# Three reorderings in a fused hybrid layer: one projection block behind a weighted sum, the entry of the up-projection written out, and the first activation blocks of the down-projection ahead of a weight fetch

## The chip, the cores and the metric

One core of one Trainium2 chip. The metric is the device time of one execution in microseconds. An execution is told apart from its span: the span runs from the first to the last instruction that the profile shows, the execution is a little longer.

## What is computed

One layer of a streaming encoder, on 512 frames of width 1024, all in float32:

```python
h = rms_norm(x, mix_norm_pre)
xa, ga, q, k, v, f_logit, g_a, g_b = split(h @ w_in)
y_a = gelu(ga) * rg_lru(causal_dwconv(xa))                   # recurrent branch, width 1280
y_b = forgetting_attention(q, k, v, f_logit + b_forget)      # 16 heads of 64
merged = sigmoid(g_a + b0) * (y_a @ w_proj_a) + sigmoid(g_b + b1) * (y_b @ w_proj_b)
x = x + rms_norm(merged @ w_out, mix_norm_post)
h = rms_norm(x, ffn_norm_pre)
gate, val = split(causal_dwconv(h @ w_up))                   # 3 taps, 2 x 3072 channels
x = x + rms_norm((gelu(gate) * val) @ w_down, ffn_norm_post)
```

## The kernel before

**Products.** Each float32 operand is split into a high part, rounded to the matmul's type, and a low part, the remainder. ACT makes the high part (a cast, `hi`), DVE the low one (a subtraction, `lo`, `sub`), and PE adds three products (high x high, high x low, low x high) in one PSUM bank. Weights come by DMA on SP's queue into a buffer `raw`, of which there are four, and go through the same split into `wh` and `wl`. Since a buffer is taken in turn, a fetch on SP waits until the split of an earlier weight has been read, and every DMA that is queued on SP behind it waits with it.

**Attention.** Heads go in eight pairs, one a turn of the loop over `p`. A pair's scores are made on PE, normalised on DVE and ACT (`normalise`), turned by PE transposes into PSUM banks (`pt`, tiles pt and pt_r, two banks a head), split (PTh on ACT, PTl on DVE), and multiplied with v (`av`). The result lies in two banks, one a head; ACT copies half (ytmp), DVE adds (y), ACT rounds (yb, index 0), DVE takes the remainder (yb, index 1). Pair p's transposes and `av` come one turn later, in turn p + 1. In the last turn PE's time is filled with `pb_part(e, ks)`: block e of the product of y_b with `w_proj_b`, for the pairs ks. For each k it is three products that read yb of pair k, and it accumulates in bank pb e.

**Up-projection.** Pairs of weight blocks, one for the gate and one for the value (block j and j + 24), of which the first three (`NU`) are computed plainly and the rest, from j = 3 on, by a seven-product scheme on halves (class `Pair`): products 1, 2, 4 read plain weight quarters, 3 another plain quarter, 5, 6, 7 sums of quarters. A plain quarter's high part mh is a cast on ACT (`plain_high`). Its low part ml is made by ACT writing minus the high part (`plain_low`), after which a DMA that POOL issues adds the raw weight in place (line 360). `sums` are subtractions on DVE (t), `sums_hi` and `sums_lo` split them (th, tl). `keep(i, ps)` copies a bank's half to SBUF on ACT (x), since it is needed in a later sum; product 3 accumulates into the half that `keep(1)` reads, and product 6 into the one that `keep(2)` reads. From j = 3 on `period` gives the order of one pair's work by hand, with the preparation of the next two pairs (`n1`, `n2`) in between. The work ahead of the first period is written out by hand too; there `p` is pair 3, `n` pair 4, and pair 5 is prepared by the first period. The three plain pairs' convolution taps (`first_tap` on ACT, `first_taps` on DVE), gelu and product (`first_glu`: gelu on ACT, yf on POOL, stored to DRAM as yd by SP) stand in between.

**Down-projection.** 42 steps in seven products by six blocks of weights, `STEPS`, each of twelve matmuls of 128x512. A step needs weights (wh_dn, wl_dn) and activations (ah, al, made from yr or q). `load_w(i)` queues the fetch of step i's weights on SP, `load_q` that of a block q of activations from yd in DRAM (128x2x256 elements, half the bytes of a weight block). Steps 0 to 5 read yr; step 6, the first of product 4, reads the first q block, which `load_22(0)` loads. The q tiles lie in a pool that is opened after the up-projection's memory is given back (`ustk.close`). `extra[i]` is a list of what is done beside step i.

**Order.** In the parts under `manual_schedule` the order on each engine is the order of the code. Elsewhere a scheduler orders each engine's instructions, by estimates of its own; in the attention it does.

Of the kernel before, what the change touches and what calls it, by code (L numbers as in the profile page):

```python
# [19 lines left out]
KD = D // P  # L20
# [43 lines left out]
def kernel(  # L64
# [274 lines left out]
    class Pair:  # L339
# [14 lines left out]

        def plain_low(self, i):

            src = self.plain_src(i)
            l = self.ml[i] = self.split_tile(i, "ml")
            act.activation(out=l, in_=src, func=AF.Copy, scale=-1.0)  # L359
            nc.gpsimd.dma_start(l, src, accum_op=ALU.add)  # L360
# [2 lines left out]
            return (self.r[0], self.r[1][:, B])[i]  # L363

        def plain_high(self, i):
            src = self.plain_src(i)
            h = self.split_tile(i, "mh")
            act.copy(h, src)
            l = self.ml.get(i)
            if l is None:  # L370
                l = self.split_tile(i, "ml")
                sub(l, src, h.bitcast(F32))
            if i == 0:
                self.w[1], self.w[2] = quarter(h, l, A), quarter(h, l, B)
            else:
                self.w[3] = quarter(h, l, A)

        def plain(self, i):
            if i not in self.ml:
                self.plain_low(i)  # L380
                self.plain_high(i)

        def sums(self, i):
            r0, r1 = self.r
            t = self.t[i] = self.st.tpool.tile([P, D], F32, tag="t", name=self.name(f"t{i}"))
            if i == 0:
                sub(t[:, A], r1[:, A], r0[:, A])
                sub(t[:, B], r1[:, B], r1[:, A])
            else:
                sub(t[:, A], r1[:, B], self.t[0][:, A])  # L390
                sub(t[:, B], r0[:, B], t[:, A])
# [566 lines left out]
    with ExitStack() as at:  # L958
# [39 lines left out]
        def normalise(pts):  # L998
            for Pt, sm in pts:
                dve.reciprocal(sm, sm)  # L1000
                for b in (3, 2, 0, 1):
                    w = P * (b + 1)
                    dve.tensor_scalar(out=Pt[:, PO[b] : PO[b] + w], in0=Pt[:, PO[b] : PO[b] + w],
                                      scalar1=sm[:, b : b + 1], scalar2=None, op0=ALU.mult)
# [25 lines left out]
        def av(p, pts):  # L1030
            y = apool.tile([P, S], F32, tag="y", name=f"y{p}", bufs=2)
            tmp = apool.tile([P, S], F32, tag="ytmp", name=f"ytmp{p}", bufs=1)
            for j in range(2):
                th, tl = pts[j]
                po = bank(f"av{2 * p + j}")
                for kb in range(NT):
                    st = vt[p][:, kb, 2 * j : 2 * j + 2, :].rearrange("p a b -> p (a b)")
                    d = slice(PTO[kb], PTO[kb] + S - kb * P)
                    pe.matmul(po[:, kb * P :], st, th[:, d], start=kb == 0, stop=False)
                    pe.matmul(po[:, kb * P :], st, tl[:, d], start=False, stop=kb == NT - 1)  # L1040
                r = slice(HD * j, HD * (j + 1))
                o = slice(HD * (1 - j), HD * (2 - j))
                act.copy(tmp[r], po[o])
                dve.tensor_tensor(out=y[r], in0=po[r], in1=tmp[r], op=ALU.add)
            yb[p] = vpools[p // 4].tile([P, 2, S], F32R, tag="vy", name=f"yb{p}")
            act.copy(yb[p][:, 0], y)
            dve.tensor_tensor(out=yb[p][:, 1], in0=y, in1=yb[p][:, 0].bitcast(F32), op=ALU.subtract)
# [3 lines left out]
        def pb_part(e, ks):  # L1051
            if e not in pb:
                pb[e] = bank(f"pb{e}")
                pbw[e] = unit(f"pb{e}", 1)
            wh, wl = pbw[e]
            for k in ks:
                mm3(pb[e], wh[:, k], wl[:, k], yb[k][:, 0], yb[k][:, 1], k == 0, k == KD - 1)
# [9 lines left out]
        for p in range(KD):  # L1067
            if p == 0:
                pq = held("q1", 1)
            now = scores(p, q, k, bias)  # L1070
            if p < KD - 1:
                bias = prep_alloc(p + 1)
            if 0 < p < KD - 1:
                pq = bank(f"q{p + 1}")
                project(pq, (unit if p > 1 else behind)(f"q{p + 1}"), hh, hl)
            elif p:
                pb_part(0, range(KD - 2))
            if prev is not None:
                pts = pt(p - 1, prev)
            if p < KD - 1:  # L1080
                pk = bank(f"k{p + 1}")
                project(pk, behind(f"k{p + 1}", 2 if p else 0), hh, hl)
                q, k = halves(pq, f"q{p + 1}"), halves(pk, f"k{p + 1}")
            else:
                pb_part(1, range(KD - 2))
            if p == 0:
                b.product(4, b.a[:, Y])
                gate_epilogue(b, "a", 0)
                gate_epilogue(b, "a", 1)
            if prev is not None:  # L1090
                av(p - 1, pts)
            normalise(now)
            prev = now
        pts = pt(KD - 1, prev)
        for e in range(2):
            pb_part(e, range(KD - 2, KD - 1))
        pb_part(2, range(KD - 1))
        av(KD - 1, pts)

# [46 lines left out]
    def up_pair(j):  # L1146
        return Pair(ups, j, (f"up{j}", f"up{j + JF}"))
# [200 lines left out]
    first_tap(1)  # L1348
    first_taps(1)
    first_tap(2)  # L1350
    p.p12()
    n.sums_hi(0)
    n.sums_hi(1)
    n.plain(1)
    p.keep(2, p.a[:, Y])
    p.add(p.a[:, X], p.a[:, X], 2)
    pairs[NU + 2] = up_pair(NU + 2)
    p.p5()
    n.sums_lo(0)
    p.keep(1, p.c[:, X])  # L1360
    n.sums_lo(1)
    first_glu(1)
    first_tap(0)
    first_taps(2)
    first_taps(0, 0)
    PRODUCTS = (1, 4, 5, 6, 7, 3, 2)
    WQ = {1: (0, 0), 2: (1, 0), 3: (1, 1), 4: 3, 5: 0, 6: 1, 7: 2}
    STEPS = [(n, m) for n in PRODUCTS for m in range(NS)]
# [51 lines left out]
    pairs.update({j: none for j in (JF, JF + 1, JF + 2)})  # L1420

    def load(j):
        if j + 3 < JF:
            pairs[j + 3] = up_pair(j + 3)
        elif j == JF - 2:
            for i in range(2):
                load_w(i)
                load_first(i)

    with man2:  # L1430
# [20 lines left out]
        y_lo(0)  # L1451
        p.product(3, p.c[:, X])
        taps(b.j, b.a, b.g)
        gelu(b.g)
        wd[1].hi()
        y_hi(1)
        glu(b.j, b.g, b.v)
        p.product(7, p.a[:, Y])
        p.add(p.c[:, Y], p.a[:, Y], 1)
# [15 lines left out]
            load_w(i + 1)  # L1475
        down_step(1)
        down_step(2)
        load_w(7)
        prep(4)
        gelu(p.g)  # L1480
        glu(p.j, p.g, p.v)
# [72 lines left out]
        extra = {i: [] for i in range(len(STEPS))}  # L1554
        at_ = {n: NS * PRODUCTS.index(n) for n in PRODUCTS}
        gpost = dpool.tile([P, D], F32, name="gpost")
        for m in range(NS):
            for i, f, a in ((1, load_22, (m,)), (6, load_q, (1, 0, m)), (12, load_q, (0, 0, m)), (19, load_12, (m,)),
                            (8, s1, (m,)), (14, s2, (m,)), (20, s3, (m,)), (26, s4, (m,))):
                extra[max(3, i + m)].append(lambda f=f, a=a: f(*a))  # L1560
        extra[5].append(lambda: nc.sync.dma_start(gpost, gains[3:4, :].partition_broadcast(P)))
        extra[9].append(lambda: act.mul(gpost[:, DH:], gpost[:, DH:], -1.0))
        extra[9].append(lambda: act.activation(out=warm, in_=epst, func=AF.Sqrt))
# [142 lines left out]
```

## Time and profile before

| | us |
|---|---|
| median of 3 runs (lowest to highest) | 915.69 (915.38 to 916.62) |
| profiled execution | 916.23 |
| its span | 914.5 |
| PE matmul busy | 904.9 (99%) |
| DVE busy | 725.6 (79%) |
| ACT busy | 601.7 (66%) |
| POOL busy | 217.6 (24%) |

The page's busy time counts a matmul from its start to an end that is modelled, so that neighbours overlap: the start of one row and the start of the next say how fast PE goes. The TensorE clock was granted fully (0.998 on the mean). In the timeline a row is: start, us from there to the last end, engine, line, operation, output<-inputs, how many; in square brackets the idle time of the engine ahead of it and what ended that. PE is the matmul engine, DVE VectorE, ACT ScalarE, POOL GpSimd, SP SyncE; a "q" behind an engine's name marks its queue of DMAs.

### The profile page before, as it was taken

What the parts mean: (1) busy time and instruction counts of PE and PEld (TensorE: products, weight loads), DVE (VectorE), ACT (ScalarE), POOL (GpSimd) and SP (SyncE); (2) the same over time, 40 slices, a digit from 0 to 9 for tenths busy, and PEclk for the clock granted to TensorE, in tenths of its full rate; (3) what the DMA queues carried; (4) which work ended last, traced back from release to release, by engine and by line L of the source; (5) the groups of instructions that cost most, each with busy time, mean ns of one, the idle gap of its engine ahead of it and who ended that gap; (6) DMA issues with size and microseconds to landing.
All of it is one profiled execution on the core that took longest, in us unless ns stands there. A gap on an engine that the chain in (4) does not pass through costs nothing.

```text
span 914.5 us, 15941 instructions
## 1 busy us (share of the span) xinstructions
PE 904.9 (99%) x5906; PEld 805.5 (88%) x5906; DVE 725.6 (79%) x1197; ACT 601.7 (66%) x1041; POOL 217.6 (24%) x281
## 2 busy tenths in 40 slices
PE   9999999999999999999999999999999999999997
PEld 7988888878899998888888889999999999978886
DVE  5966369638777649888868589899999999889897
ACT  7555495433367748776754487688888888677664
POOL 4134345444111112112104100133323223100000
PEclk9999999999999999999999999999999999999999
DMA  7667689989877978444515664378889988699764
GB/s 282 238 211 209 166 204 260 252 230 196 199 168 179 208 248 272 149 143 146 177 44 176 204 186 137 93 205 207 225 218 215 240 202 213 223 378 321 245 201 148
DMA packets 72048, 187.86 MB, mean 205 GB/s; under 512 B 7265, under 2 KB 27793, under 8 KB 71586
## 3 DMA queue, kind: packets, MB, share of 16 engines
q1 hardware_dynamic: 47648, 127.72, 42.1%
q0 software_dynamic: 24176, 58.99, 30.1%
q8 instruction: 46, 0.75, 0.3%
q14 instruction: 32, 0.26, 0.1%
q10 hardware_dynamic: 146, 0.14, 0.0%
HBM read 150.69 MB, written 35.73 MB: 204 GB/s over the span
## 4 chain that ended last, share of the span: by engine, by line
PE 92%; DVE 4%; DMA 1%; issue 1%; ACT 1%; POOL 0%; DVEq 0%; POOLq 0%; ACTq 0%
PE up L416 7%; PE up L414 7%; PE up L413 7%; PE dn L1418 4%; PE dn L1416 4%; PE dn L1417 4%; PE pa L218 2%; PE ga L219 2%; PE pa L217 2%; PE ga L218 2%; PE pa L219 2%; PE ga L217 2%; PE k L217 2%; PE q L217 2%; PE pb L217 2%; PE pb L218 2%
## 5 line engine op out<-in xcount | busy, mean ns | idle before, releaser
L1298 DVE SCALAR_TENSOR_TENSOR u<-up,cpt,u 128x511 f32<-128x511 f32 x96 | 71.2, 745 | 2.6 <-ACT u L1292 0.9
L360 POOL DMA_DIRECT2D ml<-raw_up x41 | 35.2, 859 | 153.9 <-ACT ml L359 87.2
L1416 PE MATMUL dn<-wh_dn,ah 128*128 128x512 f32 (+1 forms) x180 | 67.6, 376 | 0.5 <-ACT ah L1384 0.5
L1418 PE MATMUL dn<-wh_dn,al 128*128 128x512 f32 (+1 forms) x180 | 67.7, 376 | 0.0
L1417 PE MATMUL dn<-wl_dn,ah 128*128 128x512 f32 (+1 forms) x180 | 67.5, 375 | 0.0
L413 PE MATMUL up<-sh,th 128*128 128x256 f32 x252 | 60.3, 276 | 0.0
L414 PE MATMUL up<-sl,th 128*128 128x256 f32 x252 | 60.3, 276 | 0.0
L175 DVE TENSOR_TENSOR wl_dn<-raw_dn,wh_dn 128x1024 fp32r<-128x1024 f32 x42 | 51.5, 1226 | 8.7 <-ACT wh_dn L172 8.7
L172 ACT CAST wh_dn<-raw_dn 128x1024 fp32r<-128x1024 f32 x42 | 44.1, 1050 | 18.7 <-issue 6.9
L324 DVE TENSOR_TENSOR tl<-t,th 128x1024 fp32r<-128x1024 f32 x42 | 51.0, 1217 | 0.0
L1292 ACT ACTIVATE u<-up,cpt 128x512 f32<-128x512 f32 x48 | 36.9, 778 | 21.1 <-PE up L416 11.1
L413 PEld LDWEIGHTS up<-sh,th 128*128 128x128 f32 x252 | 47.3, 188 | 0.0
L414 PEld LDWEIGHTS up<-sl,th 128*128 128x128 f32 x252 | 47.3, 188 | 0.0
L395 ACT CAST th<-t 128x1024 fp32r<-128x1024 f32 x42 | 43.7, 1044 | 4.2 <-DVE t L324 1.2
L1306 POOL TENSOR_TENSOR yf<-u,u 128x512 f32<-128x512 f32 x23 | 29.9, 1298 | 64.0 <-issue 48.0
L413 PE MATMUL up<-h2h,mh 128*128 128x256 f32 x168 | 40.3, 277 | 0.0
L414 PE MATMUL up<-h2l,mh 128*128 128x256 f32 x168 | 40.2, 276 | 0.0
L1416 PEld LDWEIGHTS dn<-wh_dn,ah 128*128 128x128 f32 x180 | 33.9, 188 | 6.9 <-ACT ah L1384 0.9
L1418 PEld LDWEIGHTS dn<-wh_dn,al 128*128 128x128 f32 x180 | 33.9, 188 | 6.9 <-DVE al L324 0.8
L1417 PEld LDWEIGHTS dn<-wl_dn,ah 128*128 128x128 f32 x180 | 33.9, 188 | 6.1
L416 PE MATMUL up<-sh,tl 128*128 128x256 f32 x252 | 38.9, 276 | 0.0
L432 DVE TENSOR_TENSOR up<-up,x 128x256 f32<-128x256 f32 x63 | 27.1, 432 | 14.1 <-PE up L416 9.0
(711 smaller groups left out, 3244.4 us busy)
## 6 DMA issues: line engine op xcount, KB each, us to landing
raw_up<-in_w_up_dram SPq DMA_DIRECT2D x48, 512.0 KB, 5.6
td<-in_w_down_dram POOLq DMA_DIRECT2D x36, 512.0 KB, 6.1
raw_dn<-td SPq DMA_DIRECT2D x24, 512.0 KB, 5.8
B<-cnd POOLq DMA_DIRECT2D x16, 640.0 KB, 5.4
ml<-raw_up POOLq DMA_DIRECT2D x20, 512.0 KB, 5.3
raw_dn<-in_w_down_dram SPq DMA_DIRECT2D x18, 512.0 KB, 4.3
raw_wo<-in_w_out_dram SPq DMA_DIRECT2D x16, 512.0 KB, 4.1
td<-td POOLq DMA_DIRECT2D x12, 512.0 KB, 11.3
```

Of the source, the lines that this page charges most:

```text
L172: act.copy(self.wh, self.raw)
L175: engine.tensor_tensor(out=self.wl, in0=self.raw, in1=self.wh.bitcast(F32), op=ALU.subtract)
L217: pe.matmul(dst, ah, bh, start=first, stop=False)
L218: pe.matmul(dst, ah, bl, start=False, stop=False)
L324: dve.tensor_tensor(out=out, in0=a, in1=b, op=ALU.subtract)
L413: pe.matmul(dst, wh[:, k], ah[:, k], start=first and k == 0, stop=False, skip_group_check=True)
L414: pe.matmul(dst, wh[:, k], al[:, k], start=False, stop=False, skip_group_check=True)
L416: pe.matmul(dst, wl[:, k], ah[:, k], start=False, stop=k == KH - 1, skip_group_check=True)
L1298: dve.scalar_tensor_tensor(out=c[:, s:], in0=ps[:, : S - s], scalar=col(C_CFW + 3 * e + j), in1=c[:, s:], op0=ALU.mult, op1=ALU.add)
L1416: pe.matmul(d[:, x], ah[:, k, tok], wh[:, k, x], start=first, stop=False, skip_group_check=True)
L1417: pe.matmul(d[:, x], ah[:, k, tok], wl[:, k, x], start=False, stop=False, skip_group_check=True)
L1418: pe.matmul(d[:, x], al[:, k, tok], wh[:, k, x], start=False, stop=last, skip_group_check=True)
```

## The change

It has three parts.

1. The attention's last turn: of the six blocks of pb 1 (pairs 0 to 5) that stood ahead of `av(6)`, the last, that of pair 5, now stands behind it, ahead of the transposes of pair 7. And the blocks of pair 6 for pb 0 and pb 1 take the four products with yb's high part first, and the two with its low part last.

```diff
             else:
-                pb_part(1, range(KD - 2))
+                pb_part(1, range(KD - 3))
...
             if prev is not None:
                 av(p - 1, pts)
+            if p == KD - 1:
+                pb_part(1, range(KD - 3, KD - 2))
             normalise(now)
             prev = now
         pts = pt(KD - 1, prev)
+        i = KD - 2
         for e in range(2):
-            pb_part(e, range(KD - 2, KD - 1))
+            for w in pbw[e]:
+                pe.matmul(pb[e], w[:, i], yb[i][:, 0], start=False, stop=False)
+        for e in range(2):
+            pe.matmul(pb[e], pbw[e][0][:, i], yb[i][:, 1], start=False, stop=False)
         pb_part(2, range(KD - 1))
```

On PE at the end of the attention (pb1 is bank 1 of the product with `w_proj_b`, yb4 and yb5 the pairs 4 and 5, av12 and av13 the two heads of pair 6) there stood before:

```order
L219 MATMUL pb1_5401<-yb4_4998,wl_pb1_5191 128x512
L217 MATMUL pb1_5401<-yb5_5251,wh_pb1_5190 128x512
L218 MATMUL pb1_5401<-yb5_5251,wh_pb1_5190 128x512
L219 MATMUL pb1_5401<-yb5_5251,wl_pb1_5191 128x512
L1039 MATMUL av12_5428<-PTh12_5381,v6_1285 128x512
```

and now, from the last matmuls of pair 6's second head to its reading of the block:

```order
L1044 MATMUL av13_5436<-PTh13_5391,v6_1285 128x128
L1045 MATMUL av13_5436<-PTl13_5392,v6_1285 128x128
L217 MATMUL pb1_5401<-yb5_5251,wh_pb1_5190 128x512
L218 MATMUL pb1_5401<-yb5_5251,wh_pb1_5190 128x512
L219 MATMUL pb1_5401<-yb5_5251,wl_pb1_5191 128x512
```

The three products of pair 5 moved behind the sixteen of `av(6)`; the transposes of pair 7 follow them. The scheduler also moved, on ACT and on DVE, the cast and the subtraction that make yb of pair 6 ahead of the first cast (PTh) and the first subtraction (PTl) of pair 7's probabilities.

2. The up-projection's entry: the weight loads of the sixth and seventh of all pairs after the third's (j = 5 and 6) are issued together, ahead of the first store of yf; the gelu and taps of plain pairs 1 and 0 and the low halves of pair 4's sums stand ahead of `p12` of pair 3; and the first plain quarter of pair 5, its high and low part, stands ahead of `keep(1)` of pair 3, its first sums at the end. `plain_low`, `plain_high` and `sums` return at once where their work is done already, and the first period loads nothing.

```diff
-    p.p12()
     n.sums_hi(0)
     n.sums_hi(1)
     n.plain(1)
-    p.keep(2, p.a[:, Y])
-    p.add(p.a[:, X], p.a[:, X], 2)
-    pairs[NU + 2] = up_pair(NU + 2)
-    p.p5()
+    for j in (NU + 2, NU + 3):
+        pairs[j] = up_pair(j)
+    m = pairs[NU + 2]
     n.sums_lo(0)
-    p.keep(1, p.c[:, X])
     n.sums_lo(1)
     first_glu(1)
     first_tap(0)
+    p.p12()
+    p.keep(2, p.a[:, Y])
+    p.add(p.a[:, X], p.a[:, X], 2)
+    m.plain_low(0)
+    m.plain_high(0)
+    p.p5()
+    p.keep(1, p.c[:, X])
     first_taps(2)
     first_taps(0, 0)
+    m.sums(0)
...
     def load(j):
-        if j + 3 < JF:
+        if NU < j < JF - 3:
             pairs[j + 3] = up_pair(j + 3)
```

On ACT at that place (x_3 are the kept halves of pair 3, u the taps and gelus, ml_5 and mh_5 the low and high part of pair 5's first quarter) there stood before:

```order
L420 COPY x_3_6838<-up_6804 128x256
L420 COPY x_3_6860<-up_6845 128x256
L1302 ACT_TABLE_LOAD
L1302 ACTIVATE u_6792<-u_6792 128x512
L1292 ACTIVATE u_6868<-up_6286,cpt 128x512
L1292 ACTIVATE u_6870<-up_6311,cpt 128x512
L420 COPY x_3_6890<-up_6804 128x256
L359 ACTIVATE ml_5_6892<-raw_up_6841 128x1024
L368 CAST mh_5_6907<-raw_up_6841 128x1024
```

and now:

```order
L1313 ACT_TABLE_LOAD
L1313 ACTIVATE u_6792<-u_6792 128x512
L1303 ACTIVATE u_6829<-up_6286,cpt 128x512
L1303 ACTIVATE u_6831<-up_6311,cpt 128x512
L425 COPY x_3_6858<-up_6833 128x256
L361 ACTIVATE ml_5_6861<-raw_up_6813 128x1024
L372 CAST mh_5_6864<-raw_up_6813 128x1024
L425 COPY x_3_6879<-up_6866 128x256
L425 COPY x_3_6902<-up_6833 128x256
```

The gelu and its neighbours moved ahead of the first kept copy, and pair 5's quarter from behind the third kept copy to between the first and the second. The order of PE and of POOL is the same as before.

3. The down-projection's entry: the first three q blocks are queued on SP ahead of `load_w(7)` and of the fetch behind it, instead of beside step 3; and the high parts of step 1's weights and activations stand ahead of a gelu on ACT.

```diff
-        gelu(b.g)
         wd[1].hi()
         y_hi(1)
+        gelu(b.g)
         glu(b.j, b.g, b.v)
...
         down_step(2)
-        load_w(7)
         prep(4)
...
+        for m in range(3):
+            load_22(m)
+        load_w(7)
         for m in range(NS):
...
-                extra[max(3, i + m)].append(lambda f=f, a=a: f(*a))
+                if f is not load_22 or m > 2:
+                    extra[i + m].append(lambda f=f, a=a: f(*a))
```

On SP's queue (raw_dn_0 to raw_dn_3 with td are the weights of steps 6 to 9, q_0 to q_2 the activations of steps 6 to 8) there stood before:

```order
L166 DMA raw_dn_0_9690<-td_0_100 128x1024
L166 DMA raw_dn_1_9718<-td_1_101 128x1024
L166 DMA raw_dn_2_9757<-td_2_102 128x1024
L1490 DMA q_0_9779<-yd_6766 128x2x256
L1490 DMA q_1_9781<-yd_6767 128x2x256
L1490 DMA q_2_9783<-yd_6768 128x2x256
```

and now:

```order
L166 DMA raw_dn_0_9690<-td_0_100 128x1024
L1505 DMA q_0_9753<-yd_6766 128x2x256
L1505 DMA q_1_9755<-yd_6767 128x2x256
L1505 DMA q_2_9757<-yd_6768 128x2x256
L166 DMA raw_dn_1_9759<-td_1_101 128x1024
L166 DMA raw_dn_2_9763<-td_2_102 128x1024
```

The three q blocks moved ahead of the weights of steps 7 and 8. Nothing else differs between the two programs on any engine.

More of the change, by code (lines that the diff above doesn't have):

```diff
@@ L355, in plain_low @@
         def plain_low(self, i):
+            if i in self.ml:
+                return
             src = self.plain_src(i)
@@ L365, in plain_high @@
         def plain_high(self, i):
+            if 1 + 2 * i in self.w:
+                return
             src = self.plain_src(i)
@@ L378, in plain @@
         def plain(self, i):
-            if i not in self.ml:
-                self.plain_low(i)
-                self.plain_high(i)
+            self.plain_low(i)
+            self.plain_high(i)
         def sums(self, i):
+            if i in self.t:
+                return
             r0, r1 = self.r
```

## The prediction

> **What bounds the kernel now.** I read the page first, then who waits for whom on PE, then the timeline of PE around each wait, then the engines that PE waits for there. The page:
>
> ```profile
> PE 904.9 (99%) x5906; PEld 805.5 (88%) x5906; DVE 725.6 (79%) x1197; ACT 601.7 (66%) x1041; POOL 217.6 (24%) x281
> ```
>
> PE is busy for 904.9 of 914.5 us, so no other engine's speed is worth anything unless PE waits for it. The view of waits on PE lists, among five, the three that lie in the places the change touches (columns: total us, times, longest):
>
> ```profile
> PE dn L1416 <- ACT ah L1384: 0.5, 1, 0.5
> PE pt L1015 <- DVE y L1044: 0.4, 1, 0.4
> PE up L416 <- DMA ml<-raw_up: 0.3, 1, 0.3
> ```
>
> That is 1.2 us in all. It is less than what is lost: a PE row's end is modelled, and after a wait the next rows start late too. So I take starts: what a stretch took from start to start, against the same instructions undisturbed. The span is 914.5 us, the execution 916.23, so 1.73 us lie outside the span; nothing in the change reaches them.
>
> **Part 1, the attention's end.** PE, from pair 6's transposes (first two rows, then the step after them) to those of pair 7:
>
> ```profile
> 460.15 0.71 PE L1015 MATMUL pt<-ident,P 64*128 64x64 f32 x16
> 461.53 0.50 PE L217 MATMUL pb<-yb,wh_pb 128*128 128x512 f32 x1
> 461.87 0.39 PE L218 MATMUL pb<-yb,wh_pb 128*128 128x512 f32 x1
> 468.12 0.27 PE L1040 MATMUL av<-PTl,v 128*128 128x128 f32 x1
> 468.32 0.71 PE L1015 MATMUL pt<-ident,P 64*128 64x64 f32 x16
> 469.79 0.59 PE L1015 MATMUL pt<-ident,P 64*128 64x64 f32 x11 [0.45 <-DVE y L1044]
> 470.55 0.73 PE L217 MATMUL pb<-yb,wh_pb 128*128 128x512 f32 x2
> 472.19 0.40 PE L217 MATMUL pb<-yb,wh_pb 128*128 128x512 f32 x1
> ```
>
> Forty transposes took 461.53 - 460.15 = 1.38 us for pair 6 and 470.55 - 468.32 = 2.23 for pair 7: 0.85 lost, because the second head's bank was still being read by DVE's y. The six products behind them took 472.19 - 470.55 = 1.64; one 0.34 (461.53 to 461.87) and five at 0.23 (795.29 to 795.52, below) are 1.49: 0.15 lost. The moved block is three products of 0.23, 0.69 us. It leaves its old place, so the weighted sum and the y chain start 0.69 earlier, and stands between the last av and the transposes, where PE waited. One more change of shape costs 0.34 - 0.23 = 0.11. Gain: 0.85 + 0.15 - 0.11 = **0.9 us**, if the waits are covered. Counted from the last av (468.12), y was there at +1.61 to +1.67 (the transposes went on at 469.79). The second head now comes at 0.20 + 0.69 + 0.11 + half of 1.38 = +1.69: just covered; missing it by 0.1 costs 0.1. The next is the rounded y:
>
> ```profile
> 469.76 0.62 ACT L1046 CAST yb<-y 128x512 fp32r<-128x512 f32 x1
> ```
>
> It ends at +2.26, and the first product that reads it comes at 0.20 + 0.80 + 1.38 = +2.38. The low half is DVE's next step, some 0.7 us after it, and is now read only after four products (0.34 + 3 x 0.23 = 1.03 us): covered. What is put behind on ACT and DVE is one cast and one subtraction of pair 7's probabilities; their av stands behind the 21 products of pb 2 (21 x 0.23 = 4.8 us), so they cost nothing; without that cover each would cost its own 0.6 to 0.7.
>
> **Part 2, the up-projection's entry.**
>
> ```profile
> 606.12 0.62 PE L416 MATMUL up<-sh,ml 128*128 128x256 f32 x4
> 606.58 0.28 PE L413 MATMUL up<-h2h,mh 128*128 128x256 f32 x1
> 607.93 0.74 PE L416 MATMUL up<-h2h,ml 128*128 128x256 f32 x4 [0.29 <-DMA ml<-raw_up]
> 608.51 0.28 PE L413 MATMUL up<-h2h,mh 128*128 128x256 f32 x1
> ```
>
> Four products take 0.46 (606.12 to 606.58), so the eight from 606.58 end at 607.50 at the latest, and the ml products would start there: 0.43 lost, and 608.51 - 607.93 - 0.46 = 0.12 behind it. The ml tile comes by an accumulating transfer that POOL issues, beside two weight loads that SP issued just before:
>
> ```profile
> 598.60 0.83 SPq L346 DMA_DIRECT2D raw_up<-in_w_up_dram  x2
> 599.56 0.89 POOL L360 DMA_DIRECT2D ml<-raw_up  x1 [1.49 <-ACT ml L359]
> ml<-raw_up POOLq DMA_DIRECT2D x1, 512.0 KB, 8.3
> ```
>
> 8.3 us from 599.56 is 607.9. In the changed order ACT writes ml right after the first kept copy, so:
>
> ```profile
> 592.97 0.37 ACT L420 COPY x<-up 128x256 f32<-128x256 f32 x1 [4.47 <-PE up L416]
> 598.18 1.08 ACT L359 ACTIVATE ml<-raw_up 128x1024 fp32r<-128x1024 f32 x1
> 599.14 1.06 ACT L368 CAST mh<-raw_up 128x1024 fp32r<-128x1024 f32 x1
> 595.60 0.28 PE L413 MATMUL up<-sh,mh 128*128 128x256 f32 x1
> ```
>
> ml ends about 593.3 + 1.1 = 594.4, POOL issues then, and even 8.3 us later is 602.7, 4.8 us early; the two loads, no longer behind a store that waits for POOL, go earlier still. Gain: **0.55 us**. The price is the second kept copy, now behind ml and mh: 592.97 + 0.37 + 0.96 + 0.96 (ml to mh in the rows) = 595.26, ending by 595.63. Product 3 writes the bank it reads and starts at 595.60 (last row), so this cover is exact: 0 to 0.2 us for PE, nothing taken as likeliest. The table load, gelu and two taps go into the 4.47 us that ACT stood idle; before, they lay between 592.97 and 598.18 with three copies of 0.37 and a wait on PE, so they are under 598.18 - 592.97 - 1.11 = 4.1 us and cost nothing (the excess, if they outgrew the hole). The two low halves move into time in which DVE, too, waited for that first copy. The sixth pair's first subtractions stand a few steps earlier on DVE, ahead of an addition that has to wait for PE anyway. The store of yf, now behind two loads on SP, is read back only in the down-projection.
>
> **Part 3, the down-projection's entry.** Two places on PE:
>
> ```profile
> 794.54 0.39 PE L1417 MATMUL dn<-wl_dn,ah 128*128 128x512 f32 x1
> 794.95 0.50 PE L1418 MATMUL dn<-wh_dn,al 128*128 128x512 f32 x1
> 795.29 0.40 PE L1416 MATMUL dn<-wh_dn,ah 128*128 128x512 f32 x1
> 795.52 0.39 PE L1417 MATMUL dn<-wl_dn,ah 128*128 128x512 f32 x1
> 808.02 0.39 PE L1418 MATMUL dn<-wh_dn,al 128*128 128x512 f32 x1
> 808.89 0.50 PE L1416 MATMUL dn<-wh_dn,ah 128*128 128x512 f32 x1 [0.49 <-ACT ah L1384]
> 810.19 0.39 PE L1417 MATMUL dn<-wl_dn,ah 128*128 128x512 f32 x1
> ```
>
> First: 794.54 to 795.52 is 0.98 for three starts of 0.23: 0.29 lost, to al of step 1. Its chain:
>
> ```profile
> 791.15 0.63 ACT L1302 ACTIVATE u<-u 128x512 f32<-128x512 f32 x1 [2.26 <-DVE u L1298]
> 792.75 1.53 DVE L175 TENSOR_TENSOR wl_dn<-raw_dn,wh_dn 128x1024 fp32r<-128x1024 f32 x1 [0.89 <-ACT wh_dn L172]
> 794.22 0.68 DVE L324 TENSOR_TENSOR al<-yr,ah 128x512 fp32r<-128x512 f32 x1
> ```
>
> The weight and activation casts of step 1 (about 1.5 us) stood behind a gelu for which ACT had idled 2.26 us; ahead of it they fill that hole, the gelu is not late, and DVE starts 0.89 earlier: al at 794.0 instead of 794.9, wanted at 794.77. Gain **0.29**.
>
> Second: 808.02 to 810.19 is 2.17 for five starts of 0.23 (1.15): **1.0 us** lost, to step 6, whose activations are the first q block:
>
> ```profile
> 797.32 0.59 SPq L166 DMA_DIRECT2D raw_dn<-td  x1
> 799.32 0.33 SPq L166 DMA_DIRECT2D raw_dn<-td  x1
> 802.91 1.84 SPq L1490 DMA_DIRECT2D q<-yd  x3
> 808.22 0.62 ACT L1384 CAST ah<-q 128x512 fp32r<-128x512 f32 x1 [3.16 <-DMA q<-yd]
> DMA to landing us min/median/max: 5.2/5.9/7.3
> DMA to landing us min/median/max: 5.0/6.2/7.1
> ```
>
> (The last two rows are q's and the weights' in this stretch.) q left SP at 802.91, behind three fetches (the first two are shown) of which the second and third wait for raw buffers. Behind the first alone it can leave at 797.32 + 0.59 = 797.9, and lands at the latest 7.3 later, 805.2: three us before ACT got it. The price is the two fetches behind it. The second, for step 7, moves from 799.3 to 797.9 + 1.84 = 799.8 and has three blocks more ahead of it on its queue. They are half its size each (256 KB beside 512); taken at the 2 us by which successive fetches could leave here (797.32, 799.32), they add about 2 us. It lands at 799.8 + 6.2 + 2 = 808.0; cast and split, by the longest rows of such shapes shown here (1.06, 1.53), end at 810.6. Step 6 starts at 808.25 less the 0.29 won before, step 7 twelve products (2.7) later, and wants the split at its second product, 810.9: covered by 0.3.
>
> The Trainium skill's page "DMA: Bandwidth & Descriptors", section "Queues, rings and completion order", speaks against this edit: on each DMA engine the descriptors of one queue are consumed in the order of its ring, so nothing lets the weights overtake the q blocks. By that rule alone step 7's weights land by all three blocks later, which is the 2 us taken above; no row of this kernel shows the two in this order.
>
> **Sum.** 0.9 + 0.55 + 0.29 + 1.0 = 2.75. Three covers are thin (y, the second kept copy, step 7), so I take 0.15 off: 2.6 us. 916.23 - 2.6 = 913.6 for the profiled execution. The runs' median, 915.69, lies 0.54 under it: **913.1**. Nothing later takes it back: PE has no listed wait from 810 to its end, and what it then waits for is only its own order.
>
> **Rivals.**
> - *Only the listed idle comes back*: 0.45 + 0.29 + 0.49 = 1.2 us, 914.5. For it: PE's rows show no more idle. Against: starts slip by more at every one of them. 0.11.
> - *One cover fails*: the largest term, 1.0, or 0.9, is replaced by the next wait (y late by the block's own 0.7, or step 7's weights): 2.75 - 0.95 = 1.8, 913.9. 0.17.
> - *SP stops at the q blocks* (ends slower). They lie in memory that the up-projection held. In the trace they left at 802.91, without showing whether they could have gone sooner. If not, the fetch of step 7 leaves at 802.91 + 1.84 = 804.75, 5.4 later than it did, and every later fetch is queued behind. 804.75 + 6.2 to 7.1, + 2.6 = 813.6 to 814.5 for split weights, wanted at 810.9: PE loses 2.7 to 3.6 at step 7, keeps the loss of 1.0 at step 6 and loses up to 2 more at the next steps, whose fetches bunch up. With 1.75 won elsewhere against 2.7 to 5.6 lost: 0.95 to 3.85 slower, middle 918.1. It decides once q leaves later than about 798.3, where the cover of 0.3 ends. Against it: step 1 of the down-projection, which stands behind the last up product on PE, is there at 794.54, so the tiles were read by then. 0.06.
> - *It doesn't do what it says*: the order of instructions shows it does; 0.01.
>
> The forecast itself: 0.65. **Chances.** 0.2% is 1.83 us, about what a measurement of this kernel can tell from no change; faster by more means under 913.86. The forecast and half of the failed cover: 0.73. Same: the other half, the listed idle, the start of the blocked queue: 0.21. Slower: 0.06. **Range**: down to 915.69 - 2.75 - 0.5 (three runs spread by 1.2) = 912.4, up past the listed idle's 914.5 to 914.6.
>
> **What would show it.** Right: in the view of waits on PE no pt from DVE y, no up from ml, no dn from ah; transposes of pair 7 in about 1.4 us; q leaving SP before 800. Wrong: a wait of up on ACT x at product 3 (part 2's price), of dn on wh_dn or wl_dn at step 7 (part 3's), SP idle ahead of q (the slower rival), or a PE end that moved by 1.2 only.

## The result, and the profile after

Twenty-two runs of the changed kernel have a median of 914.88 us (913.99 to 916.61). Twenty-two of the kernel before, taken beside them, have 916.70 (914.90 to 918.51). The ratio is 0.9979, 95% interval 0.9973 to 0.9985: 1.9 us faster, between 1.4 and 2.5. I had forecast 2.6 us faster and 913.1 us, in a range of 912.4 to 914.6. The direction was right. The time lies 0.3 us above the range, for two reasons of different kinds: the base from which I counted, 915.69, was 1.0 us under what the kernel before takes on the median of more runs, and the sum was 0.7 too large.

The profiled execution took 915.62 us, its span is 913.8 us. The page's first row, and the whole view of waits on PE:

```profile
PE 904.4 (99%) x5906; PEld 805.5 (88%) x5906; DVE 726.0 (79%) x1197; ACT 601.6 (66%) x1041; POOL 218.9 (24%) x281
```

```profile
PE xa L585 <- POOL ident masks.py:199: 1.5, 1, 1.5
PE tr_p L245 <- DVE xn L611: 1.2, 1, 1.2
```

The three waits that the change aims at are gone: no pt on y, no up on ml, no dn on ah. Both rows that are left belong to the first 15 us, where the change does nothing. And yet this execution is only 0.6 us shorter than the profiled one of before (916.23), and so is its span. So the view of waits doesn't say where the time went. What does is a comparison of starts: the time from the start of PE's matmul number a to that of number b, set against the same in the first profile of before. Both programs have 5906 matmuls, in the same order but for the three of part 1 that moved and the six behind pair 7's transposes, so the numbers match at the ends of the stretches. For the two first profiles:

| stretch of matmuls, and what lies in it | before, us | after less before, us |
|---|---|---|
| 0 to 100, the start | 18.84 | +2.46 |
| 100 to 2700 | 427.58 | 0.00 |
| 2700 to 2895, part 1 | 24.97 | -0.86 |
| 2895 to 3420 | 95.63 | -0.03 |
| 3420 to 3640, plain up-projection | 25.91 | -0.98 |
| 3640 to 3780, part 2 | 16.59 | -0.45 |
| 3780 to 3850 | 7.97 | +0.15 |
| 3850 to 5370 | 174.38 | 0.00 |
| 5370 to 5410, step 1 (part 3) | 8.52 | -0.19 |
| 5410 to 5436, steps 3 to 5 | 5.91 | +0.33 |
| 5436 to 5460, step 6 (part 3) | 6.50 | -1.06 |
| 5460 to 5905 | 93.33 | 0.00 |

Two large rows, the start and the plain up-projection, are in no part of the change. They say that two profiles can't be subtracted without more of each. At the start, ACT's fourth piece of x (first row before, second row after) came 1.7 us later, and everything behind it:

```profile
6.83 0.63 ACT L593 ACTIVATE xn<-xt 128x512 f32<-128x512 f32 x1 [0.56 <-DMA xt<-in_x_dram]
```

```profile
8.54 0.63 ACT L598 ACTIVATE xn<-xt 128x512 f32<-128x512 f32 x1 [2.21 <-DMA xt<-in_x_dram]
```

In the plain up-projection PE waits for nothing in either, but goes at another pitch (the time from one start to the next). The view by windows counts the rows of PE in 25 us, before from 569 and after from 570 us:

```profile
569.00:594.00 25.00, 25.00 (x215) 1.00 0.37 85
```

```profile
570.00:595.00 25.00, 25.00 (x223) 1.00 0.47 108
```

215 matmuls against 223, at a granted clock of 1.00 in both: 117.8 ns from start to start against 113.3.

Now the three places. **Part 1**, PE's timeline after: the block of pair 5 between the last av and the transposes, then the two high parts (line 1105).

```profile
469.88 0.27 PE L1045 MATMUL av<-PTl,v 128*128 128x128 f32 x1
469.98 0.45 PE L217 MATMUL pb<-yb,wh_pb 128*128 128x512 f32 x1
470.83 0.71 PE L1020 MATMUL pt<-ident,P 64*128 64x64 f32 x16
471.50 0.76 PE L1020 MATMUL pt<-ident,P 64*128 64x64 f32 x16
472.31 0.50 PE L1105 MATMUL pb<-yb,wh_pb 128*128 128x512 f32 x1
```

```profile
470.80 0.69 DVE L1049 TENSOR_TENSOR y<-av,ytmp 64x512 f32<-64x512 f32 x1 [0.25 <-ACT ytmp L1048]
471.52 0.62 ACT L1051 CAST yb<-y 128x512 fp32r<-128x512 f32 x1 [0.76 <-DVE y L1049]
```

The forty transposes took 472.31 - 470.83 = 1.48 us instead of 2.23, and the six products behind them (472.31 to 473.79) 1.48 instead of 1.64. The second y ended at 471.49, 1.61 behind the last av, and the second head's transposes began at 471.50: the cover of y was as thin as forecast, and cost the 0.1 that the prediction gave for missing it. The rounded y ended at 472.14, in time for 472.31.

**Part 2**, ACT's second kept copy and PE's product 3:

```profile
595.79 0.37 ACT L425 COPY x<-up 128x256 f32<-128x256 f32 x1
```

```profile
595.80 0.50 PE L421 MATMUL up<-sh,tl 128*128 128x256 f32 x3
596.22 0.38 PE L418 MATMUL up<-sh,mh 128*128 128x256 f32 x1
596.44 0.28 PE L419 MATMUL up<-sl,mh 128*128 128x256 f32 x1
596.55 0.28 PE L418 MATMUL up<-sh,mh 128*128 128x256 f32 x1
```

The copy ends at 596.16. Product 3's first matmul starts 0.07 late and its second 0.11 more (0.22 instead of 0.11): 0.18 lost, at the upper end of the 0 to 0.2 that I had given and then set to nothing. In two later profiles of this order, with the slow pitch ahead of it, 0.07 to 0.08 is lost.

**Part 3.** The q blocks left SP at 798.95 and PE passes from step 5 (line 1434) to step 6 without a gap:

```profile
798.95 2.06 SPq L1505 DMA_DIRECT2D q<-yd  x3
801.11 0.55 SPq L166 DMA_DIRECT2D raw_dn<-td  x1
```

```profile
808.46 0.39 PE L1434 MATMUL dn<-wh_dn,al 128*128 128x512 f32 x1
808.69 0.39 PE L1432 MATMUL dn<-wh_dn,ah 128*128 128x512 f32 x1
```

But at step 4 there is a loss that before did not have (0.45 from start to start instead of 0.23, and 0.11 behind it):

```profile
803.12 0.40 PE L1433 MATMUL dn<-wl_dn,ah 128*128 128x512 f32 x1
803.57 0.50 PE L1434 MATMUL dn<-wh_dn,al 128*128 128x512 f32 x1
803.90 0.40 PE L1432 MATMUL dn<-wh_dn,ah 128*128 128x512 f32 x1
```

It leads back to POOL and DVE. The last product yf on POOL before (first row), and after (second), with DVE's rows of after:

```profile
791.92 1.30 POOL L1306 TENSOR_TENSOR yf<-u,u 128x512 f32<-128x512 f32 x1 [7.43 <-issue]
```

```profile
792.21 2.23 POOL L1317 TENSOR_TENSOR yf<-u,u 128x512 f32<-128x512 f32 x1 [7.43 <-issue]
792.07 1.22 DVE L175 TENSOR_TENSOR wl_dn<-raw_dn,wh_dn 128x1024 fp32r<-128x1024 f32 x1
793.20 1.79 DVE L324 TENSOR_TENSOR al<-yr,ah 128x512 fp32r<-128x512 f32 x1
```

Read in order they take turns: DVE's wl started first and took its usual 1.22 us; POOL's yf, begun 0.14 later, ended 1.15 us after it; al, which takes 0.68 elsewhere, ended 0.55 after yf. The two engines didn't share, one waited for the other. Before, they took turns the other way round: yf had started first and took 1.30, and wl of step 1 took 1.53 instead of 1.22. That row stands in the prediction, which reads nothing from it. The Trainium skill, page "SBUF — State Buffer", section "SBUF: two separate sides", says that VectorE and GpSimd have one port pair in common, which is an exclusive lock: whichever instruction starts first holds it, a VectorE one with two SBUF inputs among them, and the other blocks. The trace agrees: 0.93 us on yf and 1.1 on al, one after the other. SP stores yf and has the fetch of a later weight behind that store:

```profile
793.24 0.33 SPq L1307 DMA_DIRECT2D yd<-yf  x1
```

```profile
794.47 0.33 SPq L1318 DMA_DIRECT2D yd<-yf  x1
795.47 0.61 SPq L166 DMA_DIRECT2D raw_dn<-in_w_down_dram  x1
```

```profile
800.60 1.05 ACT L172 CAST wh_dn<-raw_dn 128x1024 fp32r<-128x1024 f32 x1 [1.95 <-DMA raw_dn<-in_w_down_dram]
```

The first row is before, the others after: 1.2 us later, of which 0.3 is the whole stretch's (matmul 5370 starts at 793.36 and at 793.66) and 0.9 is yf's. The weight is step 4's, and ACT idled 1.95 us for it.

### The profile page after: what moved, and what is told of

Same layout as the page of the kernel before. It is cut to its first block, busy times and chain, and to the rows that moved or that the text cites. A ratio compares the mean times of both kernels' runs of the same rounds, so it can differ in the third digit from the quotient of the medians.

```text
span 913.8 us, 15945 instructions
## 1 busy us (share of the span) xinstructions
PE 904.4 (99%) x5906; PEld 805.5 (88%) x5906; DVE 726.0 (79%) x1197; ACT 601.6 (66%) x1041; POOL 218.9 (24%) x281
## 4 chain that ended last, share of the span: by engine, by line
PE 96%; DVE 1%; DMA 1%; ACT 1%; SPq 0%; issue 0%; DVEq 0%; ACTq 0%
PE up L421 7%; PE up L419 7%; PE up L418 7%; PE dn L1434 4%; PE dn L1432 4%; PE dn L1433 4%; PE pa L217 2%; PE ga L218 2%; PE ga L217 2%; PE pa L219 2%; PE pa L218 2%; PE ga L219 2%; PE k L217 2%; PE q L217 2%; PE wo L1151 2%; PE pb L217 2%
## 5 line engine op out<-in xcount | busy, mean ns | idle before, releaser
L998 ACT ACTIVATE P<-P,mx 128x384 f32<-128x384 f32 (+3 forms) x64 | 35.2, 553 | 4.2 <-DVE mx L993 3.3
```

## The experiments

**My theory** after this: each part acts at its own place; part 2 costs 0.1 to 0.2 at product 3; the gelu half of part 3 pays with the POOL lock; the rest is chance. **The rivals** are in the expectations. Each time is set against the kernel before, in runs taken beside it; places are set against its first profile, unless another is named. First the parts alone.

**Part 1 alone.** The diffs of the parts are those of "The change", cut here to a few lines; dots mark the cuts.

```diff
-                pb_part(1, range(KD - 2))
+                pb_part(1, range(KD - 3))
...
+            if p == KD - 1:
+                pb_part(1, range(KD - 3, KD - 2))
...
```

> The kernel before with part 1 alone (the block of pair 5 behind the sixth pair's weighted sum, high parts of yb first). Theory, that each part acts at its own place: PE's stretch from the first product ahead of that weighted sum to the blocks behind pair 7's transposes shrinks by 0.86 us, as in the changed kernel; the wait of pt on y is gone; the waits of 0.3 on ml and of 0.5 on ah of step 6 stay; no wait of a dn product at step 4. Time 0.9 us under before. Rival, that the gain at the attention's end is given back by later stages: the same wait gone, but the end of PE moved by under 0.3 against its position at the attention's start. Also seen here: in the changed kernel the 128x256 products between 568 and 597 us went at 113.3 ns, before at 117.8. If part 1 is what sets that, it is 113.3 here; if it is left to chance, either.

915.69 us against 916.66; ratio 0.9987 (0.9977 to 0.9997). At its place -0.82 us, and nothing comes back later. The pitch stayed at 117.8 ns, so it isn't part 1 that sets it. One thing was not expected: at 607 us PE lost 0.1 instead of 0.56, although part 2 was not in.

**Part 2 alone.**

```diff
...
+    m.plain_low(0)
+    m.plain_high(0)
     p.p5()
     p.keep(1, p.c[:, X])
...
+    m.sums(0)
...
```

> The kernel before with part 2 alone (the up-projection's entry). Theory: the wait on ml at 607.93 is gone (0.55 us), but two small ones come in its place, one of about 0.1 at the first matmul of product 3, behind the kept copy on ACT, and one of about 0.14 some ten us later, at the next ml of pair 5, whose accumulating transfer is issued just behind two weight loads: net 0.33 us earlier from the entry to 620 us (without the change of pitch). Rival (the prediction's sum): 0.55, with neither of the two. Time 0.3 (rival 0.55) under before.

916.93 us against 916.66; ratio 0.9999 (0.9988 to 1.001). In its profile the entry is 0.45 shorter than in the first profile of before, with the loss at product 3; the second small loss is not there. The time shows no gain: 0 lies inside the interval, and so does 0.55.

**The gelu half of part 3 alone.**

```diff
-        gelu(b.g)
         wd[1].hi()
         y_hi(1)
+        gelu(b.g)
```

> The kernel before with the first half of part 3 alone: step 1's high parts ahead of the gelu, q blocks where they were. Theory: the gelu's product yf runs on POOL while DVE makes al of step 1; the two hold each other up (yf about 2.2 us instead of 1.3, al about 1.8 instead of 0.7), so al gains only 0.2 at step 1, and SP's store of yf and all behind it leave 1.2 us later; a wait of 0.3 at step 4's second product, and q later by 0.4, so that the wait at step 6 grows: PE's end 0.3 to 0.5 us LATER than before, measured from the last up products. Rival, that the wait at step 4 in the changed kernel is due to the q blocks on the queue: no wait at step 4 here, step 1's wait gone, the gain of 0.2 to 0.3 used up in front of step 6: PE's end unchanged.

916.81 us against 916.66; ratio 0.9999 (0.9989 to 1.001). POOL's yf took 2.23 and al 1.79 again; step 1 gained 0.20. Both expectations on step 4 were too simple: it lost 0.07. Step 6 lost 0.67 more than before, but not because q left later: its transfer took 6.0 us from issue to landing, against 5.2 in the first profile of before. So PE's end came 0.54 later, where the theory had 0.3 to 0.5 and the rival nothing; most of it is the transfer's. The times show neither loss nor gain.

**The q blocks alone.**

```diff
...
+        for m in range(3):
+            load_22(m)
+        load_w(7)
...
```

> The kernel before with the second half of part 3 alone: the three q blocks ahead of the weights of step 7, gelu where it was. Theory: q leaves SP at about 797.9, the wait at step 6 (1.0 us) is gone and nothing takes its place, no wait at step 4: PE's end 1.0 us earlier than before. Rival, that the q blocks hold up the queue: a wait of 0.3 at step 4 or one at step 7, and a gain of 0.7 or less.

915.80 us against 916.66; ratio 0.9988 (0.9978 to 0.9997). Step 6: -1.06, no wait at step 4 or 7. The theory holds and this rival falls. Here, with part 2 not in, the wait on ml was larger than ever:

```profile
PE up L416 <- DMA ml<-raw_up: 0.7, 1, 0.7
```

Then the changed kernel, with single things undone or altered.

**Without the gelu half.**

```diff
+        gelu(b.g)
         wd[1].hi()
         y_hi(1)
-        gelu(b.g)
```

> The changed kernel with the first half of part 3 undone (gelu ahead of step 1's high parts again), all else as changed. Theory: yf on POOL takes 1.3 us and al 0.7 again, SP's store leaves 1.2 us earlier; the wait at step 4 (0.33) is gone, the one of 0.2 (0.3 with what follows) at step 1 is back: PE's end from the last up products on is the same as in the changed kernel within 0.15, so this half is worth nothing. Rival (the prediction's sum): undoing it loses 0.29.

914.28 us against 915.92; ratio 0.9977 (0.9964 to 0.9989). No loss at step 4, step 1's 0.2 back: from the first up product of this stretch to the end 0.14 us less than in the changed kernel's first profile, within the 0.15 of the theory. Against the mean of its three profiles (below) it is 0.03 less: this half is worth nothing.

**The last yf but one on DVE.**

```diff
-        (dve if j == JF - 1 else pool).tensor_tensor(out=y, in0=g, in1=v, op=ALU.mult)
+        (dve if j >= JF - 2 else pool).tensor_tensor(out=y, in0=g, in1=v, op=ALU.mult)
...
-        glu(b.j, b.g, b.v)
         p.product(7, p.a[:, Y])
         p.add(p.c[:, Y], p.a[:, Y], 1)
         p.add(p.c[:, X], p.c[:, X], 0)
+        glu(b.j, b.g, b.v)
```

> The changed kernel, with the last but one product yf (gelu times value) made by DVE instead of POOL, behind the two additions of kept halves, as the last one already is. Theory, that POOL's product and DVE's al hold each other up: al of step 1 takes 0.7 us and is there by 794.5, no wait at step 1 and none at step 4; the store of yf leaves SP about 1.5 us earlier; PE's end 0.4 us earlier than in the changed kernel, measured from the last up products. Rival, that al was late for DVE's own work: the 0.7 us that yf adds on DVE come out at al, the wait at step 1 grows by 0.5.

914.61 us against 915.92; ratio 0.9983 (0.9972 to 0.9995). DVE's timeline:

```profile
790.26 0.69 DVE L1317 TENSOR_TENSOR yf<-u,u 128x512 f32<-128x512 f32 x1
790.87 1.22 DVE L175 TENSOR_TENSOR wl_dn<-raw_dn,wh_dn 128x1024 fp32r<-128x1024 f32 x1
792.01 0.68 DVE L324 TENSOR_TENSOR al<-yr,ah 128x512 fp32r<-128x512 f32 x1
```

With 0.69 us more work on DVE, al is shorter by 1.1. Step 1 is 0.32 shorter than before, and steps 3 to 5 lose nothing: 0.48 us better there than the changed kernel's first profile, where the theory had 0.4. So the taking of turns is the cause, and the prediction's 0.29 for this edit is to be had without it. By the times alone this program and the changed kernel (ratios of 0.9983 and 0.9979 to before) can't be told apart.

**This, and the kept copy ahead of mh.** The diff shows what comes on top.

```diff
     m.plain_low(0)
-    m.plain_high(0)
     p.p5()
     p.keep(1, p.c[:, X])
+    m.plain_high(0)
```

> As the one with yf on DVE, and at the up-projection's entry the second kept copy on ACT ahead of the high part of pair 5's first quarter instead of behind it. Theory: the 0.1 us that PE loses at product 3's first matmul is gone too, so that the entry gains 0.1 more; together 0.5 us under the changed kernel's time, 2.3 to 2.6 under before. Rival, that this loss is not the copy's: it stays.

914.02 us against 915.92; ratio 0.9977 (0.9963 to 0.9990). PE passes into product 3 without a gap, so that the loss there was the copy's (this profile has the slow pitch, where the loss is 0.07 to 0.08):

```profile
594.52 0.63 PE L421 MATMUL up<-sh,tl 128*128 128x256 f32 x4
595.00 0.28 PE L418 MATMUL up<-sh,mh 128*128 128x256 f32 x1
595.11 0.28 PE L419 MATMUL up<-sl,mh 128*128 128x256 f32 x1
```

By its places this is the best version, 0.6 us under the changed kernel's first profile; the runs can't tell it from the changed kernel. Against before it is 0.9 to 3.4 us faster, which holds the 2.3 to 2.6 of the theory and less.

**The eighth pair's loads behind the store.**

```diff
-        load()
+        if p.j != 4:
+            load()
         epilogue(b, "a", 3)
+        if p.j == 4:
+            load()
```

> The changed kernel, with the two weight loads that it issues at about 608.0 us (the eighth pair's) put behind the next store of yf on SP's queue, so that the accumulating transfer that POOL issues at 608.1 goes alone. With these loads beside it that transfer took 9.6 us in the changed kernel and 9.2 with part 2 alone; in four profiles where the loads left 1.5 to 2.5 us behind it, 5.4 to 5.7. Theory, that the loads hold it up: 5 to 6 us here, and no late start of PE at 618 (0.1 to 0.14). It may cost elsewhere, since the eighth pair's weights come four us later. Rival, that another transfer does: 9 us again.

One run, 915.81 us. The transfers of ml issued at 608.14 (changed kernel, first) and 608.54 (here), from issue to landing:

```profile
ml<-raw_up POOLq DMA_DIRECT2D x1, 512.0 KB, 9.6
```

```profile
ml<-raw_up POOLq DMA_DIRECT2D x1, 512.0 KB, 4.9
```

So two loads issued at its side double this transfer: one run without them, seven profiles with them (9.2 to 9.7 us). The late start at 618 is gone. It did cost elsewhere: 0.25 us at 622.86, where a product started late.

**The same programs again.** Two more profiles of each kernel, unchanged.

> The kernel before once more, for a second profile of the same program. Theory, that chance transfers and states set a good part of what one profile shows: against the first profile, the start (PE's first 100 matmuls) differs by 0 to 2.5 us, the pitch of the 128x256 products between 568 and 596 us is 113 or 118 ns, the transfer of ml that PE waited for at 607.9 takes anything from 7.5 to 9 us, so that the loss there is anything from 0 to 1.0; but the losses at pair 7's transposes (0.85), at step 1 (0.29) and at step 6 (0.9 to 1.7) are there again. Rival: the profile repeats within 0.1 us at every one of these places.

> A third profile of the kernel before; the same two expectations.

> The changed kernel once more. Theory: the 2.2 us of yf on POOL and the 1.8 of al on DVE, the 0.1 at product 3 and the 9 us of the ml transfer at 608 are there again, since they follow from the order; the wait at step 4 (0.33 in the first profile) is there only if the fetch of step 3's weights, which leaves 1.2 us later than before, takes 5 us rather than 4. Start and pitch differ by chance. Rival, that the wait at step 4 follows from the order too: there again, 0.3.

> A third profile of the changed kernel; the same two expectations.

914.75 and 916.86 us before; 915.96 and 914.00 after. What follows from the order came again, within 0.1: the 0.85 at pair 7's transposes, the loss at step 1, the 2.23 and 1.79 us of yf and al, the 9.5 us of the ml transfer at 608 with the loads at its side. What did not:

- The start: -0.26 and +0.96 against the first profile of before; +0.11 and +0.22 for the two of after, where the first had +2.46.
- A stretch of the attention's gates, +1.53 in one of before and +1.76 in one of after, with this wait, in no part of the change:

```profile
PE ma L413 <- DVE ma L432: 1.0, 1, 1.0
```

- The pitch from 568 to 596 us: 113 in both new profiles of before, 118 and 113 in those of after. Over all fourteen profiles it was slow in six and fast in eight, in either order.
- The wait on ml, which part 2 was to remove: gone in both new profiles of before. In the six profiles with the old order PE's loss follows the length of this transfer: none at 7.5, 7.6 and 7.6 us (the first and the last are the new profiles of before), 0.1 at 7.9, 0.56 at 8.3, 1.0 at 8.8. Rows of the third profile of before, and of the q blocks alone:

```profile
ml<-raw_up POOLq DMA_DIRECT2D x1, 512.0 KB, 7.6
```

```profile
ml<-raw_up POOLq DMA_DIRECT2D x1, 512.0 KB, 8.8
```

- The loss at step 6 in the old order, 1.06 in the first profile of before: 0.90 and 0.75 in the new ones, the second under the expected 0.9 to 1.7.
- The loss at step 4 of the changed order: 0.33, 0.03 and 0.27 in its three profiles, none with the late loads. The fetch of step 4's weights (795.47 above; the expectation calls them step 3's) took 5.1 us from issue to landing in the two with the loss, 4.0 to 4.3 in the others with yf held up. The rival for it (that it follows from the order alone) falls: it came where yf was held up and this transfer was slow. With yf not held up the slowest took 4.8, and PE lost nothing.

## Why the prediction was right and wrong

All fourteen profiles by place, each against the first one of before; "old" and "new" is the order at that place:

| place | old order there, us | new order there, us | difference of the means | forecast |
|---|---|---|---|---|
| part 1 | -0.01 to 0.01 (6 profiles) | -0.79 to -0.86 (8) | -0.83 | -0.9 |
| part 2 | 0, -0.65, -0.65, -0.46, -0.65, +0.52 | -0.45 to -0.51 (7) | -0.15 | -0.55 |
| step 1 | -0.01 to 0.03 (7) | -0.15 to -0.21 (5) | -0.2 | -0.29 |
| steps 3 to 5 | -0.01 to 0.02 (7) | 0.33, 0.03, 0.27, 0.07, -0.01 | +0.13 | 0 |
| step 6 | 0, -0.16, -0.31, 0.03, 0.04 (and 0.67 with the gelu moved) | -1.06 (8) | -1.0 | -1.0 |

The differences add up to 2.0 us, and the runs gave 1.9 (1.4 to 2.5). Two steps of the prediction failed. The base, 915.69, was 1.0 us too low, and this alone puts the time outside the range: counted from 916.70, the same range would have run up to 915.6. And in the sum two terms were too large: part 2 stood at 0.55 and was worth 0.15, the first half of part 3 stood at 0.29 with nothing against it, and 0.2 was won and 0.13 lost. (The four terms as printed add up to 2.74 and not 2.75; nothing hangs on it.) The prediction's steps, one by one:

- *Starts instead of waits* was right. The rival by which only the listed idle comes back (1.2 us) falls: part 1 alone and the q blocks alone gave 0.82 and 1.06 at their places where the view of waits listed 0.4 and 0.5.
- *Part 1* was right to 0.1, in its mechanism and its two thin covers: the one of y was missed at the price named for it, the one of the rounded y held.
- *Part 2* failed. The 0.55 was read from one profile, at a wait that a transfer of 8.3 us ends. (Of the 0.65 between this row's first number and the lowest, 0.56 is the wait and 0.09 the slow pitch.) The mechanism was right: in eight profiles of the new order the wait is never there. But with the old order it is there in two of six in that size or more, and in four it costs 0.1 or nothing. What the order removes is worth 0.3 on the mean, and the price that I set to nothing was 0.18 in the changed kernel's first profile and some 0.15 on the mean of seven.
- *Part 3, first half*: the cover named there (no late gelu) held. What I left out was POOL. The gelu's successor on POOL used to run beside DVE's idle 0.89 us; when I gave that hole to DVE, I took it from POOL. That idle time stood in the prediction, as a gain. In all seven profiles in which yf starts first, wl of step 1 takes 1.53 to 1.55 us; in the five in which wl starts first it takes 1.22, and yf 2.23.
- *Part 3, second half* was right in its gain, 1.0 us: q away at 798.95, step 7's weights there in time. In the rows of after those weights reached ACT at 807.91, where I had estimated 808.0:

```profile
807.91 1.05 ACT L172 CAST wh_dn<-raw_dn 128x1024 fp32r<-128x1024 f32 x1 [1.78 <-DMA raw_dn<-td]
```

  That these agree is luck. The q blocks left 1.05 us later than the 797.9 of the prediction (0.3 of it the whole stretch's, the rest the late store of yf), and so past the 798.3 from which the slower rival was to count; the weights left at 801.11 instead of 799.8. But they took 6.7 us and not 8.2. The eight profiles with the q blocks ahead have 6.4 to 7.3 for this fetch, five with the old order 5.0 to 5.8 (6.7 in the one with the gelu moved): the blocks ahead cost about 1 us, not 2. The cover was 1.4 us and not 0.3: the split of these weights ended at 810.23, and PE wanted it at 811.63.

  The rule that spoke against the edit, in the Trainium skill's page "DMA: Bandwidth & Descriptors", section "Queues, rings and completion order", is that each DMA engine consumes descriptors in ring order. The same sentence there lets a later one finish its write before an earlier one, so "nothing lets the weights overtake the q blocks" was more than it states. Here they did not overtake: the q blocks landed at 805.2 to 806.6, the weights at 807.8, late enough for ACT to idle 1.78 us, which the cover held. The slower rival, SP stopping at the q blocks, falls.
- *One cover fails* (1.8 us, 913.9) was the nearest case by size, but only by luck: the largest terms stood, and several small ones were lost.
- *The base* failed. I took the median of three runs for the kernel's time and gave its side of the range 0.5 us. Over 22 runs the kernel before spreads from 914.90 to 918.51, and its median is 916.70 there, 916.66 in the 35 runs beside the first four experiments and 915.92 in the 29 beside the next four: the base itself moves by 0.8 us from set to set. One profile couldn't show this: the first 100 matmuls take 18.84 us there, near the shortest of the fourteen. From 916.70 the same 2.6 give 914.1, which lies in the range.

What stays open: what sets the pitch of 113 or 118 ns. The granted clock doesn't show it, and neither part 1 nor the order of the entry decides it. The fourteen profiles do show when it changes. Between matmuls 3412 and 5270 PE goes over to 117.8 only right behind an interruption: the transposes ahead of the plain up-projection, or a start that comes 0.18 to 1.0 us after the one before instead of 0.11. It comes back to 113.3 only behind a product of `sh` and `sl` with a plain quarter (mh), whose starts are uneven, 113 to 120 ns, in every profile. In between it holds. Not every late start does it: the one of 0.56 in the first profile of before left it at 113.3. Why the slow pitch sometimes follows and sometimes not, no run here shows.

## What to carry to other kernels

A wait that a transfer ends is a draw: price it from several profiles of the same program. Here one such wait cost anything from 0 to 1.0 us in six profiles, another from 0.75 to 1.1 in five. A wait that ends on an engine's own instructions repeated within 0.03 us and can be priced from one. And when an edit fills an engine's hole, look at what ran on its neighbours in that hole, not only at what ran on the engine: here a subtraction on DVE and a product on POOL could only take turns, and by the places in the profile moving the product to the busier engine was the cheaper way.

## What the runs showed of the hardware

- A DVE subtraction and a POOL product, both with two SBUF inputs, ran one after the other: 1.30 became 2.23 us, 0.68 became 1.79 (in all five profiles with this order). With the product first, the subtraction of weights behind it took 1.53 to 1.55 instead of 1.22 (in all seven).
- 128x256 matmuls ran at 113.3 or at 117.8 ns from start to start over 25 us, in the same program, at a granted clock of 0.998 to 0.999: 0.98 us over 220 matmuls. The slow pitch began only behind an interruption (fourteen profiles).
- An accumulating transfer of 512 KB took longer, the nearer two plain loads of 512 KB were issued to it (fourteen profiles, up to 645 us): 4.9 us with the loads 5.0 us behind it (one transfer), 4.7 to 6.0 with the two 1.3 to 4.2 us behind (35), 5.5 with the first 1.0 to 1.1 behind (2), 6.2 to 7.2 with the first 0.70 to 0.98 behind (4), 8.0 to 9.1 with the first 0.3 to 0.6 behind (7), 9.2 to 9.7 with one 0.1 ahead and one 0.35 behind (7). With two issued 0.5 and 1.0 us ahead it took 7.5 to 8.8 (6).
- The start, PE's first 100 matmuls, took 18.6 to 21.3 us in fourteen profiles of programs that are the same there. In the longest, a load of x let ACT wait 1.7 us longer.
